# Attention scores of two heads on 64 partitions each: six products for a pair of tiles in place of four

## The chip, the cores and the metric

The kernel runs on one core of one Trainium2 chip. The metric is the device time of one execution in microseconds (us). The time before is 910.82 us, the median of three runs (909.99 to 911.43). One further execution was profiled; all views of the profile and the trace are of that one.

The engines are called as the profile calls them: PE (TensorE, matrix products; PEld is its weight load, which overlaps the products), DVE (VectorE), ACT (ScalarE), POOL (GpSimd) and SP (SyncE, which issues most DMAs). A line such as L827 is line 827 of the kernel before.

## What is computed

One encoder block over 512 tokens of width 2048: a normalised, modulated input `h`, one input projection, two token mixers side by side (dilated attention with 16 heads of 64, and a chunked gated linear attention, GLA), gates, an output projection and a last normalisation. The change touches the scores of the attention. Cut to that, the reference is:

```python
aq, ak, av = aq.reshape(hs), ak.reshape(hs), av.reshape(hs)      # 16 heads x 64
for window, dilation in ((128, 1), (512, 4), (2048, 16)):
    o_p, lse_p = dilated_window_attention(aq, ak, av, rel_bias, window, dilation)
# in it: s = q . k * 64 ** -0.5 + bias; s = where(mask, s, -1e30); p = softmax(s); o = p . v
mix_w = softmax(stack(lses))
att = einsum('pbsh,pbshe->bshe', mix_w, stack(outs))
```

The kernel folds the three patterns into one softmax: masks, bias and the multiplicity of a key are one additive row for each head (`grow`), from which a tile `g` is read at a stride.

## The kernel before, in words

**Precision.** A float32 operand is split into a high part, rounded to the product's format (fp32r), and a low part, the remainder. A product of two split operands is three products: high x high, low x high, high x low (`three`, L227 to L230).

**Stages.** First the modulation and the projection of the values, of GLA's queries and of the first two pairs of attention heads (until about 185 us). Then four projection units, "qk2", "qk4", "qk6" (queries and keys of the next four heads each) and "gk" (GLA's keys), L1255 to L1260. Beside each unit's products runs the attention of four heads, that is two pairs, whose queries and keys the stage before made. After about 440 us follow GLA, the gates and the output projection; the change does not touch those.

**Order of the work.** PE's order is the program's order, written out by hand. A unit (`unit`, L1125) has 64 ticks; a tick is one `three` of 512 columns. A list of side items, each with a place between 0 and 1, is walked along, and an item is issued when its place times 64 is reached. The other engines' order is made by the framework's scheduler from priorities, side items first.. SP works its queue of DMAs in order, so that a DMA that waits holds up those behind it.

**The attention's items** (`attention`, L798). A tile is one head `h` and one block `i` of 128 queries against 416 keys; a unit has 16 tiles. Three kinds of item:

- `score(h, i)`: two products into a PSUM tile `s` (L819, L820); two operations on DVE that add the bias and keep the running minimum (L827; the queries carry the minus sign); the exponential with its sum on ACT (L831); the reciprocal on DVE (L834); the scaling on POOL (L842). Between the minima and the reciprocal DVE gets one piece of unrelated "side work" (`beside`, L784): a sum of tokens (L1194 to L1218) or half a bias of the values (L964, L327).
- `turn(h, i)`: three transposes on PE (L857), a copy on ACT (L861) and a subtraction on DVE (L862) make the high and low part in a tile `pt`; a fourth small transpose (L870) follows for odd blocks, with L875 and L877.
- `values(h, e)`: eight products (L886) for two blocks, a copy on ACT (L889), an addition on DVE (L893).

Scores run two tiles ahead of turns, turns two ahead of values. All 40 items of a unit lie evenly on 0.8 of it, from 0.185 on (`ATT_AT`, L110), the first two and the last moved a little.

**PSUM.** Five tiles carry the tag `pj` (the projection, and L870), three the tag `pa`. Scores, turns and values draw their tiles from these three in turn: the next comes free only when the one three places back has been read.

**Queries and keys** (`qk_evict`, L757). The projection leaves two heads' queries in one PSUM tile, 64 partitions each, and their keys in another. The kernel makes for each head a tile `ks` whose one half of the partitions holds the keys' high part and whose other half holds their low part (L766, L767), and tiles `qh` and `ql` with the queries' high and low part in both halves: one half is written by ACT or DVE (L773, L775), the other is a copy by DMA across partitions (L774, L777). So a product of 128 rows is `qh . (kh + kl)`, and two products give all four terms. Keys 0 to 255 stand a second time at 512 to 767, copied by DMA (L770), since a block's window of 416 keys runs over the end.

**Bias rows.** `g_load` (L804) fetches one head's `g` (384 KB) into one of the two tiles of tag `g`; the next head's is asked for in the second score of the present head.

Of the kernel before, what the change touches and what calls it, by code (L numbers as in the profile page):

```python
# [10 lines left out]
F32 = mybir.dt.float32  # L11
# [7 lines left out]
P = 128  # L19
# [170 lines left out]
def block_kernel(ctx: ExitStack, tc: tile.TileContext, a: dict):  # L190
# [566 lines left out]
    def qk_evict(p, psq, psk):  # L757

        for j in range(2):
            own = slice(64 * j, 64 * j + 64)
            oth = slice(64 - 64 * j, 128 - 64 * j)
            ks = key_tile(2 * p + j)
            src = psk[own].rearrange("p (c a) -> p a c", a=2)
            act(by_parity(ks, own), src, AF.Copy)  # L766
            tt(by_parity(ks, oth), src, by_parity(ks.bitcast(F32), own), op=ALU.subtract)  # L767
# [30 lines left out]
    def attention(pairs):  # L798

        tiles = [(2 * p + j, i) for p in pairs for j in range(2) for i in range(4)]  # L800
# [8 lines left out]
        def score(h, i):  # L809
            def go():  # L810
                if h % 8 == 0 and i == 0:
                    cat[h // 8] = B8(f"cat{h // 8}", [4, 512])
# [6 lines left out]
                mm(ps[:, :NK], qh[:, q], ks[:, k], start=True, stop=False)  # L819
                mm(ps[:, :NK], ql[:, q], ks[:, k], start=False, stop=True)  # L820
# [12 lines left out]
                with tc.issue_after(held) if held else nullcontext():  # L833
                    nc.vector.reciprocal(st[:, 2:3], st[:, 1:2])  # L834
# [939 lines left out]
```

## Time and profile before

| what | value |
|---|---|
| median of three runs | 910.82 us |
| the profiled execution, its own time | 910.26 us |
| its span (first to last instruction) | 908.5 us |
| PE busy | 894.6 us, 98% of the span |
| DVE busy | 727.5 us, 80% |
| ACT busy | 492.9 us, 54% |
| mean granted PE clock | 0.997 of full speed |
| first and last score product | 194.8 and 435.1 us |
| moved by DMA | 241.30 MB, mean 266 GB/s |

A product is pipelined: its record lasts longer than the time after which the next one starts, so the pitch between starts, not the duration, is what a product costs in a full stream. In a row by group the numbers behind the bar are busy us, mean ns of one, and the idle time ahead of it with what ended it.

### The profile page before, as it was taken

Reading aid. Unit: us, or ns where it says so; the run is one execution under the profiler, and the core shown is the slowest. Engines: PE = TensorE matmul, PEld = TensorE weight load, DVE = VectorE, ACT = ScalarE, POOL = GpSimd, SP = SyncE. Lnnn points to the kernel's source line nnn. Section 1 sums busy time; section 2 is a strip of 40 time slices with the busy share of each in tenths; the row PEclk is TensorE's granted clock in tenths of the full one; section 3 lists DMA queues with packets and bytes.
Section 4 is the critical chain, followed back from the end, with each engine's and each line's share of the span. In section 5 each row is a group of like instructions: output and inputs, shape, how many; then the busy total and the mean of one; then the engine's idle time right before and its main releaser. Section 6 shows DMA issues by size and latency. Waiting matters only on the chain.

```text
span 908.5 us, 12576 instructions
## 1 busy us (share of the span) xinstructions
PE 894.6 (98%) x4295; PEld 746.9 (82%) x4295; DVE 727.5 (80%) x1235; ACT 492.9 (54%) x855; POOL 113.8 (13%) x203
## 2 busy tenths in 40 slices
PE   8999999999999999999999999999999999999996
PEld 6888888888888888888878888888888888888884
DVE  7988799878879888888659668495787559797797
ACT  5553533565655655655658554373654238455464
POOL 0000000023312222222100101111120100000001
PEclk9999999999999999999999999999999999999998
DMA  9999498588688898997878979778796987887863
GB/s 348 402 413 400 181 356 316 167 247 229 202 267 250 239 254 243 240 283 209 275 242 257 319 199 312 210 232 273 230 282 200 278 288 277 294 286 254 298 233 143
DMA packets 64203, 241.30 MB, mean 266 GB/s; under 512 B 8357, under 2 KB 10693, under 8 KB 54537
## 3 DMA queue, kind: packets, MB, share of 16 engines
q1 hardware_dynamic: 57378, 198.18, 61.1%
q0 software_dynamic: 6464, 42.01, 20.0%
q8 instruction: 34, 0.56, 0.2%
q10 hardware_dynamic: 296, 0.30, 0.1%
q14 instruction: 31, 0.25, 0.1%
HBM read 224.64 MB, written 51.47 MB: 304 GB/s over the span
## 4 chain that ended last, share of the span: by engine, by line
PE 92%; DVE 3%; ACT 2%; DMA 1%; issue 1%; SPq 0%; DVEq 0%; ACTq 0%
PE ps_qk L228 5%; PE ps_qk L229 5%; PE ps_qk L230 5%; PE g L230 4%; PE g L229 4%; PE g L228 4%; PE o L886 3%; PE stb L230 3%; PE stb L228 3%; PE stb L229 3%; PE ps_ag L228 3%; PE ps_ag L230 3%; PE ps_ag L229 3%; PE ps_gv_P L228 3%; PE ps_gv_P L229 3%; PE ps_gv_P L230 3%
## 5 line engine op out<-in xcount | busy, mean ns | idle before, releaser
L327 DVE CUSTOM_DVE_ANT_0 cb<-cb,sb,c_bcond 128x2048 f32<-128x2048 f32 (+1 forms) x32 | 73.4, 2295 | 0.3 <-DMA cb<-in_wm 0.3
L842 POOL TENSOR_SCALAR p<-p,st 128x416 f32<-128x416 f32 (+2 forms) x93 | 47.3, 516 | 175.2 <-DVE st L834 133.1
L831 ACT ACTIVATE p<-p,st 128x416 f32<-128x416 f32 x64 | 41.0, 641 | 39.5 <-DVE st L827 37.1
L861 ACT ACTIVATE pt<-t 128x384 fp32r<-128x384 f32 x64 | 31.2, 487 | 31.0 <-PE t L857 30.5
L428 POOL DMA_DIRECT2D T<-in_w_o x32 | 23.1, 723 | 157.9 <-ACT V2h L492 10.8
L886 PEld LDWEIGHTS o<-pt,vv 128*128 128x128 f32 x256 | 34.4, 189 | 4.2 <-DVE pt L862 1.7
L862 DVE TENSOR_TENSOR pt<-t,pt 128x384 fp32r<-128x384 f32 x64 | 35.1, 549 | 2.5 <-ACT pt L861 2.0
L886 PE MATMUL o<-pt,vv 128*128 128x256 f32 x256 | 35.9, 283 | 0.1
L857 PEld LDWEIGHTS t<-c_ident,p 128*128 128x128 f32 x192 | 24.8, 140 | 8.6
L857 PE MATMUL t<-c_ident,p 128*128 128x128 f32 x192 | 31.3, 272 | 0.0
L827 DVE CUSTOM_DVE_ANT_0 p<-s,g 128x160 f32<-128x160 f32 x64 | 23.5, 367 | 7.2 <-PE s L820 6.3
L827 DVE CUSTOM_DVE_ANT_0 p<-s,g,st 128x256 f32<-128x256 f32 x64 | 27.6, 431 | 1.6
L327 DVE CUSTOM_DVE_ANT_0 rawg<-rawg,crow,gate 128x1024 f32<-128x1024 f32 x16 | 20.4, 1280 | 4.1 <-DMA rawg<-in_wg 4.1
L820 PE MATMUL s<-ks,ql 128*128 128x416 f32 x64 | 22.5, 352 | 0.0
L819 PE MATMUL s<-ks,qh 128*128 128x416 f32 x64 | 22.5, 352 | 0.0
L1057 ACT ACTIVATE sq<-st,sc 128x256 f32<-128x256 f32 x24 | 12.2, 506 | 18.4 <-DVE st L1047 9.9
L428 POOL DMA_DIRECT2D T3V<-in_w_gv x8 | 5.5, 687 | 126.0 <-ACT qk21h L492 119.8
L1547 POOL TENSOR_SCALAR x<-x,rn 128x512 f32<-128x512 f32 x2 | 2.3, 1164 | 148.0 <-ACT rn L1536 143.6
L327 DVE CUSTOM_DVE_ANT_0 rawg<-rawg,crow,c_bcond 128x1024 f32<-128x1024 f32 x16 | 20.3, 1279 | 0.1
L877 DVE TENSOR_TENSOR pt<-r,pt 32x128 fp32r<-32x128 f32 x64 | 17.8, 279 | 1.9 <-ACT pt L875 1.3
L428 POOL DMA_DIRECT2D T<-T x16 | 9.1, 571 | 79.9 <-ACT V8h L492 12.9
L562 ACT ACTIVATE h_hi<-xt,shift 128x512 fp32r<-128x512 f32 x16 | 11.5, 719 | 12.9 <-DVE shift L327 12.9
(1660 smaller groups left out, 3129.6 us busy)
## 6 DMA issues: line engine op xcount, KB each, us to landing
cb<-in_wm SPq DMA_DIRECT2D x31, 1024.0 KB, 9.0
T<-in_w_o POOLq DMA_DIRECT2D x32, 512.0 KB, 6.6
rawg<-in_wg SPq DMA_DIRECT2D x32, 512.0 KB, 5.8
raw_O<-in_w_o SPq DMA_DIRECT2D x32, 512.0 KB, 4.4
raw_qk<-in_w_qk SPq DMA_DIRECT2D x24, 512.0 KB, 4.6
raw_O<-T SPq DMA_DIRECT2D x24, 512.0 KB, 5.0
rawb<-in_w_sb SPq DMA_DIRECT2D x16, 512.0 KB, 5.4
rawv<-in_wv SPq DMA_DIRECT2D x16, 512.0 KB, 4.4
```

Of the source, the lines that this page charges most:

```text
L228: mm(ps, lh, rh, start=first, stop=False, skip_group_check=more)
L229: mm(ps, ll, rh, start=False, stop=False, skip_group_check=more)
L230: mm(ps, lh, rl, start=False, stop=last, skip_group_check=more)
L327: return nc.vector.tensor_tensor_reduce(out=w, in0=w, in1=with_, op0=ALU.mult, op1=ALU.add, scale=1.0, scalar=init, accum_out=dst)
L428: move = nc.gpsimd.dma_start(dst, src, max_dma_last_dim=8192, **how).ins
L827: top = nc.vector.tensor_tensor_reduce(out=t[:, lo:hi], in0=ps[:, lo:hi], in1=gt[h][:, at:at + 2 * (hi - lo) - 1:2], op0=ALU.add, op1=ALU.min,
L831: act(t, t, AF.Exp, bias=st[:, 0:1], scale=-1.0, accum_out=st[:, 1:2])
L842: last["pool"] = nc.gpsimd.tensor_scalar(to, of, st[:, 2:3], 1.0, op0=ALU.mult, op1=ALU.mult).ins
L857: nc.tensor.transpose(pk[:, kt * P:kt * P + P], t[:, first_ + kt * P:first_ + kt * P + P], ident)
L861: act(hi, src, AF.Copy)
L862: tt(lo, src, hi.bitcast(F32), op=ALU.subtract)
L886: mm(po[:, :256], vv[h // 4][:, CHUNK_OF[e][c], h % 4, :], t[:, w, c, :], start=n_ == 0 and w == 0, stop=n_ == 3 and w == 1)
```

## The change

Two heads are now worked on together. `qk_evict` splits the whole PSUM tile of 128 partitions at once: `kh`, `kl`, `qh`, `ql` hold two heads, one on each half of the partitions. The keys' second copy is made from PSUM as well. No DMA copies queries or keys any more. A score item is a pair of heads and one block: six products of 64 rows, two heads in turn, into two PSUM tiles; the product low x low is no longer computed. Then the two tiles' chains follow (`chances`, which holds L821 to L843 as before).

With it the order changes: the tiles of a unit alternate between the two heads, so there are 8 score items in place of 16 and 32 items in all; values stand ahead of turns; a tile `pt` belongs to a head's parity and no longer to a half of the blocks; both heads' bias tiles are asked for together, behind the last score of the pair before; and the two last tiles that ACT scales in place of POOL are the last blocks of heads 14 and 15.

```diff
     def qk_evict(p, psq, psk):
-        for j in range(2):
-            own = slice(64 * j, 64 * j + 64)
-            oth = slice(64 - 64 * j, 128 - 64 * j)
-            ks = key_tile(2 * p + j)
-            src = psk[own].rearrange("p (c a) -> p a c", a=2)
-            act(by_parity(ks, own), src, AF.Copy)
-            tt(by_parity(ks, oth), src, by_parity(ks.bitcast(F32), own), op=ALU.subtract)
-            both = key_pair.get(p // 2) if p % 2 else ks
-            if p % 2 == 0 or j:
-                nc.sync.dma_start(both[..., 512:768].bitcast(F32), both[..., 0:256].bitcast(F32))
-            qh, ql = T2(f"qh{p}{j}", F32R), T2(f"ql{p}{j}", F32R)
-            src = psq[own, ::-1].rearrange("p (c e) -> p e c", e=2)
-            act(by_parity(qh, own), src, AF.Copy, scale=-0.125)
-            nc.sync.dma_start(qh[oth].bitcast(F32), qh[own].bitcast(F32))
-            stt(by_parity(ql, own), src, -0.125, by_parity(qh.bitcast(F32), own),
-                op0=ALU.mult, op1=ALU.subtract)
-            nc.sync.dma_start(ql[oth].bitcast(F32), ql[own].bitcast(F32))
-            stacks[2 * p + j] = [qh, ql, ks, own]
+        kh, kl = key_tile(2 * p), key_tile(2 * p + 1)
+        every = slice(0, P)
+        src = psk.rearrange("p (c a) -> p a c", a=2)
+        act(by_parity(kh, every), src, AF.Copy)
+        tt(by_parity(kl, every), src, by_parity(kh.bitcast(F32), every), op=ALU.subtract)
+        qh, ql = T2(f"qh{p}", F32R), T2(f"ql{p}", F32R)
+        of = psq[:, ::-1].rearrange("p (c e) -> p e c", e=2)
+        act(by_parity(qh, every), of, AF.Copy, scale=-0.125)
+        stt(by_parity(ql, every), of, -0.125, by_parity(qh.bitcast(F32), every),
+            op0=ALU.mult, op1=ALU.subtract)
+        act(kh[:, 512:768], src[:, 0, :], AF.Copy)
+        tt(kl[:, 512:768], src[:, 0, :], kh[:, 512:768].bitcast(F32), op=ALU.subtract)
+        stacks[p] = [qh, ql, kh, kl]
...
-        tiles = [(2 * p + j, i) for p in pairs for j in range(2) for i in range(4)]
+        tiles = [(2 * p + j, i) for p in pairs for i in range(4) for j in range(2)]
...
-        def score(h, i):
+        def score(p, i):
             def go():
...
-                if i == 1 and h != heads[-1]:
-                    g_load(h + 1)
-                qh, ql, ks, _ = stacks[h]
+                qh, ql, kh, kl = stacks[p]
                 q = slice(P * i, P * i + P)
                 k = slice(KEYS_AT[i], KEYS_AT[i] + NK)
-                ps = PA(f"s{h}{i}")
-                mm(ps[:, :NK], qh[:, q], ks[:, k], start=True, stop=False)
-                mm(ps[:, :NK], ql[:, q], ks[:, k], start=False, stop=True)
...
+                pss = [PA(f"s{2 * p + j}{i}") for j in range(2)]
+                for n_, (l, r) in enumerate(((qh, kh), (ql, kh), (qh, kl))):
+                    for j in range(2):
+                        own = slice(64 * j, 64 * j + 64)
+                        mm(pss[j][:, :NK], l[own, q], r[own, k], start=n_ == 0, stop=n_ == 2)
+                for j in range(2):
+                    chances(2 * p + j, i, pss[j])
+                if i == 3 and p != pairs[-1]:
+                    g_load(2 * p + 2)
+                    g_load(2 * p + 3)
             return go
+
+        def chances(h, i, ps):
...
-                    if (h, i) in ((15, 2), (15, 3)):
+                if h >= 14 and i == 3:
...
         def turn(h, i):
             def go():
                 e, half = divmod(i, 2)
-                if len(pts) == e:
-                    pts.append(B8(f"pt{e}", [2, 4, 256], F32R))
+                j = h % 2
+                if len(pts) == j:
+                    pts.append(B8(f"pt{j}", [2, 4, 256], F32R))
...
-                pt, t = pts[e], pr_[h, i]
+                pt, t = pts[j], pr_[h, i]
...
         for x in range(n + 4):
-            if x < n:
-                items.append(score(*tiles[x]))
-            if 2 <= x <= n + 1:
-                items.append(turn(*tiles[x - 2]))
+            if x < n and x % 2 == 0:
+                items.append(score(tiles[x][0] // 2, tiles[x][1]))
             v = x - 4
             if 0 <= v < n and tiles[v][1] % 2 == 1:
                 items.append(values(tiles[v][0], tiles[v][1] // 2))
+            if 2 <= x <= n + 1:
+                items.append(turn(*tiles[x - 2]))
         g_load(heads[0])
+        g_load(heads[1])
```

More of the change, by code (lines that the diff above doesn't have):

```diff
@@ L831, in go @@
-                act(t, t, AF.Exp, bias=st[:, 0:1], scale=-1.0, accum_out=st[:, 1:2])
-                held = beside(top)
-                with tc.issue_after(held) if held else nullcontext():
-                    nc.vector.reciprocal(st[:, 2:3], st[:, 1:2])
-                todo_ = [(t, t)]
-                if i % 2:
-                    todo_ = [(t[:, :384], t[:, :384]), (pr_[h, i - 1][:, 64:96], t[:, 384:416])]
-                for to, of in todo_:
-                    if (h, i) in ((15, 2), (15, 3)):
-                        act(to, of, AF.Copy, scale=st[:, 2:3])
-                    else:
-                        last["pool"] = nc.gpsimd.tensor_scalar(to, of, st[:, 2:3], 1.0, op0=ALU.mult, op1=ALU.mult).ins
@@ L880, in go @@
             def go():
-                t = pts[e]
+                t = pts[h % 2]
                 po = PA(f"o{h}{e}")
```

46 lines of the change are left out of this document (29 added, 17 removed).

## The prediction

> **What bounds the kernel now.** I read the page first: the busy line, then the chain that ended last.
>
> ```profile
> span 908.5 us, 12576 instructions
> PE 894.6 (98%) x4295; PEld 746.9 (82%) x4295; DVE 727.5 (80%) x1235; ACT 492.9 (54%) x855; POOL 113.8 (13%) x203
> ...
> PE 92%; DVE 3%; ACT 2%; DMA 1%; issue 1%; SPq 0%; DVEq 0%; ACTq 0%
> ```
>
> PE is 92% of the chain. A busy PE need not be one that waits for nothing, so I went to the stage that the change touches, four units with attention beside them, from about 195 to 438 us. The first row is the stretch of one of those units in which attention items run; the sum is that of eight stretches which cover 195 to 455 us.
>
> ```profile
> 265.00:309.00 44.00, 43.97 (x240) 37.51 (x239) 39.62 (x123) 25.52 (x64) 13.12 (x25) 1.00 0.87 266
> ...
> sum 260.00, PE 259.95 PEld 221.45 DVE 217.17 ACT 153.70 POOL 68.09; mean PE 32.49 PEld 27.68 DVE 27.15 ACT 19.21 POOL 8.51
> ```
>
> The columns are length, busy PE, PEld, DVE, ACT, POOL, granted clock (1.00), DMA share and GB/s. PE idles 0.05 us in 260; DVE is next, 39.62 of 44 us, 90%. Then PE's timeline, for the pitch from one product to the next, which is what a product costs in a full stream:
>
> ```profile
> 211.31 0.35 PE L819 MATMUL s<-ks,qh 128*128 128x416 f32 x1
> 211.50 0.35 PE L820 MATMUL s<-ks,ql 128*128 128x416 f32 x1
> 211.68 0.39 PE L228 MATMUL ps_qk<-h_hi,qk23h 128*128 128x512 f32 x1
> 211.91 0.39 PE L229 MATMUL ps_qk<-h_hi,qk23l 128*128 128x512 f32 x1
> 212.14 0.39 PE L230 MATMUL ps_qk<-h_lo,qk23h 128*128 128x512 f32 x1
> 212.37 0.49 PE L857 MATMUL t<-c_ident,p 128*128 128x128 f32 x3
> 212.61 0.48 PE L228 MATMUL ps_qk<-h_hi,qk23h 128*128 128x512 f32 x1
> 212.93 0.39 PE L229 MATMUL ps_qk<-h_hi,qk23l 128*128 128x512 f32 x1
> ```
>
> A score product lasts 0.35 us but the next begins 0.185 us later (211.31 to 211.68 for two). A projection product of 512 columns has a pitch of 0.23. Three transposes cost 0.33 (212.37 to 212.93 less one 0.23), 0.11 each. So PE time in this stage is the kernel's time, both ways: each 0.185 us that the scores save or add is saved or added, unless PE then starts to wait.
>
> **The change part by part.**
>
> *The products.* A pair of score tiles (two heads, one block of 128 queries) takes four products of 128 rows now and six of 64 rows after. There are 32 such pairs: 128 products become 192. The trace has no product of 64 rows, so I bound it. If two products on different halves of the rows run side by side, a pair of tiles costs 3 x 0.185 = 0.555 us instead of 4 x 0.185 = 0.74: 32 x 0.185 = 5.9 us less. If they take turns it costs 6 x 0.185 = 1.11: 11.8 us more. I take side by side. The pitch follows the columns streamed (0.185 for 416, 0.23 for 512), and two streams that use different halves of the rows carry together what one of 128 rows carries; nothing in these rows asks for a second pass. This is the weakest step; the other end stays in the range.
>
> A measurement from the Trainium skill leans the same way: "TensorE: Matmul & The Clock Gate", in Part 3, says that matmuls in distinct row groups start about 4 ns apart and run at once. By that a pair of tiles would cost 0.555 us and a few ns. No run here shows it.
>
> *The weight loads.* Six loads of 128 columns have to fit in where four were.
>
> ```profile
> L820 PEld LDWEIGHTS s<-ks,ql 128*128 128x128 f32 x64 | 12.0, 188 | 2.7
> L1278 PEld LDWEIGHTS plr<-h_hi,lrs 128*64 128x64 f32 x3 | 0.4, 135 | 0.1
> ...
> 209.67 1.10 PE L886 MATMUL o<-pt,vv 128*128 128x256 f32 x8
> 210.61 0.40 PE L228 MATMUL ps_qk<-h_hi,qk23h 128*128 128x512 f32 x1
> ```
>
> A load is 188 ns for 128 columns and 135 for 64: 53 ns for each 64, so 107 of the 188 grow with the columns. The L886 products run at a pitch of 0.94 / 8 = 0.117 us with loads as long, so a load hides behind 0.117. Two loads one after the other need 2 x 0.107 = 0.214 for each couple, above 0.185: the gain would be 32 x (0.74 - 0.642) = 3.1 us. If loads into different halves overlap, it stays 5.9. I take 5.9 and keep 3.1 as a rival.
>
> *Changes of shape.* PE goes from 128-row products to 64-row ones and back in each of 32 rounds. The only change of shape in the trace is in the columns:
>
> ```profile
> 451.56 0.39 PE L230 MATMUL ps_gv_P<-V2l,h_hi 128*128 128x512 f32 x1
> 451.79 0.40 PE L1278 MATMUL plr<-h_hi,lrs 128*64 128x512 f32 x1
> 452.03 0.39 PE L1279 MATMUL plr<-h_lo,lrs 128*64 128x512 f32 x1
> 452.26 0.39 PE L228 MATMUL ps_gv_P<-V2h,h_hi 128*128 128x512 f32 x1
> 452.48 0.39 PE L229 MATMUL ps_gv_P<-V2h,h_lo 128*128 128x512 f32 x1
> ```
>
> To 64 columns and back the pitch stays 0.23 us. I put rows at nothing too. The other end: PE lets the tail of the last product run out at each change, 0.35 - 0.185 = 0.165 us, 64 times, 10.6 us.
>
> The Trainium skill speaks for that other end: "TensorEngine Tiling (Array Packing)", Key Properties, has it that a change of tiling mode, unlike a change of tile, drains the engine. By that rule the sum would be the second rival's below; the rows above show no drain where only the columns change.
>
> *The ring of three PSUM tiles (pa).* Score, turn and values share three tiles. Now one score item takes one; after, it takes two at once, and PE, which runs in order, stops with the projection's products queued behind it if the ring is full. There are 32 items instead of 40 in 0.8 of 64 ticks: 1.6 ticks apart, a tick being three products, 0.69 us, so 1.10 us. Where a score is followed by two turns and the next score (4 rounds of 8 in a unit, 16 in all), the next score comes 3 x 1.10 + 0.555 + 0.33 + 0.44 = 4.63 us after it and needs the second head's tile back. How long that tile is held, from DVE's timeline now:
>
> ```profile
> 259.18 1.23 DVE L476 TENSOR_TENSOR qk43l<-raw_qk,qk43h 128x1024 fp32r<-128x1024 f32 x1 [2.87 <-ACT qk43h L492]
> 260.32 0.32 DVE L827 CUSTOM_DVE_ANT_0 p<-s,g 128x160 f32<-128x160 f32 x1
> ...
> 261.09 0.08 DVE L827 DVE_READ_ACCUMULATOR2_ANT st<- 128x1 f32 x1
> 261.09 0.69 DVE L1194 TENSOR_TENSOR S<-h_hi 128x512 f32<-128x512 f32 x1
> 261.70 0.42 DVE L827 CUSTOM_DVE_ANT_0 p<-s,g 128x256 f32<-128x256 f32 x1
> 262.05 0.08 DVE L827 DVE_READ_ACCUMULATOR2_ANT st<- 128x1 f32 x1
> 262.05 0.16 DVE L834 RECIPROCAL st<-st 128x1 f32<-128x1 f32 x1
> ...
> L862 DVE TENSOR_TENSOR pt<-t,pt 128x384 fp32r<-128x384 f32 x13 | 7.1, 548 | 0.3 <-ACT pt L861 0.3
> L964 DVE CUSTOM_DVE_ANT_0 rawv<-rawv,shb 128x1024 f32<-128x1024 f32 x3 | 3.7, 1220 | 0.0
> ```
>
> Products with tail 0.555 + 0.165, the first head's two biased minima 0.85 (260.32 to 261.17), its side work 0.69 or 1.22, the reciprocal 0.16, the second head's minima 0.85: 3.3 to 3.8 us, which fits in 4.63. With an L476 (1.23) and an L862 (0.55) ahead in DVE's queue it is 5.1 to 5.6, some 0.7 over. L476 comes about once a round. I let one tight round in four meet it in full: 4 x 0.7 = 2.8 us of PE waiting. The ends are 0 and 16 x 0.7 = 11.2.
>
> *The eviction of queries and keys.* Per pair of heads four copies on ACT and four subtractions on DVE over 64 partitions become two and two over 128, and one of each over 256 elements is new.
>
> ```profile
> L767 DVE TENSOR_TENSOR ks<-ps_qk,ks 64x512 fp32r<-64x512 f32 x12 | 8.3, 689 | 0.4
> L766 ACT ACTIVATE ks<-ps_qk 64x512 fp32r<-64x512 f32 x12 | 7.1, 594 | 1.6 <-DVE ks L767 1.4
> L893 DVE TENSOR_TENSOR cat<-o,oh 64x256 f32<-64x256 f32 x5 | 2.1, 416 | 0.7 <-ACT oh L889 0.6
> L889 ACT ACTIVATE oh<-o 64x256 f32<-64x256 f32 x30 | 11.4, 381 | 11.2 <-PE o L886 10.2 <-ACT pt L875 0.3
> ...
> qh<-qh SPq DMA_DIRECT2D x16, 128.0 KB, 6.0
> ql<-ql SPq DMA_DIRECT2D x16, 128.0 KB, 7.5
> ks<-ks SPq DMA_DIRECT2D x8, 128.0 KB, 7.5
> ks<-ks SPq DMA_DIRECT2D x4, 256.0 KB, 4.9
> ```
>
> DVE saves 2 x 0.689 - 0.42 = 0.96 us a pair, ACT 2 x 0.594 - 0.38 = 0.81, times eight 7.7 and 6.5 us; here I assume that 128 partitions take the time of 64, and nothing hangs on it. 44 transfers go from SP's queue. None of it is on the path: PE does not idle at the ends of units, and the first score comes some 10 ticks into a unit, about 7 us and more after the last eviction. I count nothing for it. Gain or loss here could be a tenth or two at each of four seams, within 1 us.
>
> *The bias rows (g).* Both heads' tiles now come together, into the only two tiles of that tag, behind the last score of the pair before. In mid-unit the load waits on SP for DVE's last read, with the weight loads of the projection behind it; those are fetched two to three groups of 8 ticks ahead, over 11 us, which covers it.
>
> ```profile
> g<-grow SPq DMA_DIRECT2D x16, 384.0 KB, 5.3
> ```
>
> From that score to the next lie 5 x 1.10 + 0.555 + 0.33 + 0.44 + 2 x 0.94 = 8.7 us. The first head's tile is read by 0.72 + 0.85 = 1.6 and lands at 6.9; the second's at 3.8 + 5.3 = 9.1, and it is read about 1.6 us or more into the round. It fits by 1 us or so; without that cover each of four mid-unit changes loses 1 to 2 us. I count nothing, and the range has room for it.
>
> *Sum.* The profiled execution took 910.26 us, 1.76 around its span of 908.5; the median of the runs shown is 910.82, 0.56 above it. Span: 908.5 - 5.9 + 2.8 = 905.4; with 1.76 around it 907.2; on the footing of the median 907.7 us.
>
> **The rivals.** Each on the same footing, 910.8 before.
>
> 1. *The halves take turns*: six products at 0.185, so the change does not do what "side by side" says. 910.8 + 11.8 = 922.6; PE is then slow enough that the ring does not bind. For it: no row shows two products sharing a stream time. Against it: the pitch is a matter of columns alone. It turns slower as soon as a couple costs over 0.25 us.
> 2. *The change of rows drains PE*: 10.6 - 5.9 = 4.7 more, 915.5; the ring is not waited for, since PE drains. Against it the 0.23 us around L1278; for it that rows are not columns.
> 3. *The ring takes the place of the products*: every tight round meets a full DVE queue, 11.2 - 5.9 = 5.3 more, 916.1. For it DVE's 90%; against it the 7.7 us that DVE sheds (outside these rounds) and that a wait gives DVE time. It ends slower from 0.37 us a tight round on.
> 4. *The loads set the pitch*: 3.1 less, 2.8 of waiting back, 910.5: no difference.
>
> **How the numbers follow.** A measurement of this kernel tells about 0.2% (1.8 us) from no change. My forecast, 904.9 (nothing waits) to 909.0: 0.42. Loads: 0.13. Drain: 0.10. Ring: 0.13. Turns: 0.18. What is left, mostly lost bias loads and mixtures on the slow side: 0.04. Faster by over 0.2% has the forecast and the better part of the load case: 0.45; within 0.2% the rest of that case and a half-filled ring: 0.13; slower 0.42. Both signs hold much, so the likeliest case's own range is 904.9 to 909.0; the range that holds 8 in 10 is 904.5 to 923.5, which takes in the turns.
>
> **What would show it.** Right: score products of 64 rows that start in couples a few ns apart, couples 0.185 us apart, no gap at their edges, and PE waits of under 3 us in all before score or turn. Wrong: single starts 0.185 apart (turns); couples 0.21 apart (loads); a gap of 0.165 at each edge (drain); PE waiting for DVE's L827 ahead of a score or turn (ring) or DVE's L827 waiting for a DMA (bias rows).

## The result, and the profile after

| | before | after |
|---|---|---|
| median | 910.87 us (3 runs and those beside the change) | 945.41 us (4 runs, 943.45 to 947.77) |
| ratio | | 1.0376, 95% interval 1.0364 to 1.0389 |
| the profiled execution, its span | 910.26, 908.5 us | 944.64, 942.9 us |
| scores of the first attention unit to the values' last product | 194.8 to 446.9 us | 195.8 to 478.7 us |

The change makes the kernel slower by 34.5 us, outside the range of the prediction. The page of the kernel after, its busy line and the chain that ended last:

```profile
span 942.9 us, 12569 instructions
...
PE 908.7 (96%) x4359; PEld 736.4 (78%) x4359; DVE 719.9 (76%) x1227; ACT 487.3 (52%) x848; POOL 131.3 (14%) x202
...
PE 77%; DVE 10%; DMA 6%; issue 4%; ACT 2%; POOL 1%; DVEq 0%; ACTq 0%; SPq 0%; POOLq 0%
```

PE was 92% of the chain and is 77% now; DVE comes in with 10%. The same stretch of time as in the prediction, into which less of the unit's work now falls, by windows (length, PE, PEld, DVE, ACT, POOL, clock, DMA share, GB/s):

```profile
265.00:309.00 44.00, 41.02 (x226) 31.43 (x225) 35.45 (x112) 21.93 (x55) 17.49 (x24) 1.00 0.68 208
```

PE idles 3 us of 44 where it idled 0.03, and DVE is busy *less*, 35.45 us in place of 39.62, as is ACT (21.93, 25.52); POOL is busier (17.49, 13.12) and far from full. So no engine has become full: the engines wait for each other. The granted clock is full here. Who PE waits for, in the view of waits (us in total, times, longest):

```profile
PE r L871 <- DVE pt L879: 16.7, 12, 2.5
PE t L858 <- POOL p L843: 2.3, 2, 1.2
```

L871 is the fourth, small transpose (L870 before), L879 the subtraction that reads its tile last. The second question is what the products themselves cost. PE's timeline around one score visit, with starts in the first column:

```profile
209.66 0.40 PE L230 MATMUL ps_qk<-h_lo,qk22h 128*128 128x512 f32 x1
209.99 0.46 PE L813 MATMUL s<-ks,qh 64*128 64x416 f32 x2
210.29 0.35 PE L813 MATMUL s<-ks,ql 64*128 64x416 f32 x2
210.48 0.35 PE L813 MATMUL s<-ks,qh 64*128 64x416 f32 x2
210.76 0.50 PE L228 MATMUL ps_qk<-h_hi,qk23h 128*128 128x512 f32 x1
211.09 0.39 PE L229 MATMUL ps_qk<-h_hi,qk23l 128*128 128x512 f32 x1
```

Three couples ("x2"): the two halves do run side by side (single starts lie 3 ns apart, median of 32 visits), and the third couple follows the second after 0.19. But four gaps are longer than the pitch of their products: into the visit 0.33 (209.66 to 209.99; 0.23 before the change), first to second couple 0.30 (0.19), out of it 0.28 (0.19), and the first product behind it 0.33 (0.23). Each is 0.10 too long, 0.40 a visit.

PE's weight loads show where half of this comes from:

```profile
209.44 0.19 PEld L230 LDWEIGHTS ps_qk<-h_lo,qk22h 128*128 128x128 f32 x1
209.99 0.19 PEld L813 LDWEIGHTS s<-ks,qh 64*128 64x128 f32 x2 [0.36 <-issue]
210.10 0.19 PEld L813 LDWEIGHTS s<-ks,ql 64*128 64x128 f32 x2
...
210.75 0.19 PEld L228 LDWEIGHTS ps_qk<-h_hi,qk23h 128*128 128x128 f32 x1 [0.28 <-issue]
210.86 0.19 PEld L229 LDWEIGHTS ps_qk<-h_hi,qk23l 128*128 128x128 f32 x1
```

In the stream a load runs one product ahead of its own product (L230: load at 209.44, product at 209.66). At a change of rows it starts only together with its product, 2 ns ahead (median of 32 visits; 0.23 us ahead of a visit's first product in the kernel before). The next load follows 0.11 us later, and the second product starts that much late. This is the second and the fourth of the long gaps. For the two others, into the visit and out of it, the trace shows only that neither a load nor a product of the new shape starts sooner.

**Where the 34.4 us of span went.** I added up, from the first score product to the last values product, what each gap between PE's starts exceeds the pitch of its product in a full stream (so a score visit counts whole: its products are nothing but excess).

| us | before | after |
|---|---|---|
| score visits | 24.7 | 33.2 |
| ahead of the fourth transpose (r) | 0.0 | 19.7 |
| ahead of and between other transposes (t) | 0.4 | 3.6 |
| projection, values, rest | 3.1 | 3.1 |
| sum | 28.2 | 59.6 |

31.4 of the 34.4 lie there: 8.5 in the visits and 22.9 in waits ahead of transposes. A further 2.6 arise behind the attention, mostly in the output projection; no experiment was aimed at them and they stay open. The last 0.4 is not placed.

Of the 8.5 in the visits, about 6.6 are the long gaps less the products saved (a clean visit takes 0.98 us, the four products before took 0.77). One visit that ran at half the granted clock adds 1.0. The second visit of each of the four units adds 0.2 to 0.45, about 1.3 in all: one head's first product waits there for a `pa` tile, and starts 0.16 us after DVE has read it, four times out of four (the read ends at 197.61, the product starts at 197.76). These parts are taken against the median visit and add up only roughly.

**How the wait for r arises.** PE and the others around one such wait, from the timeline of after; in brackets the idle time and what ended it:

```profile
275.71 0.49 PE L858 MATMUL t<-c_ident,p 128*128 128x128 f32 x3
...
276.02 0.69 DVE L1212 TENSOR_TENSOR S<-S,h_lo 128x512 f32<-128x512 f32 x1
276.04 0.27 PE L871 MATMUL r<-c_ident,p 128*64 128x128 f32 x1
...
277.11 1.21 DVE L967 CUSTOM_DVE_ANT_0 rawv<-rawv,shb 128x1024 f32<-128x1024 f32 x1
277.21 0.53 ACT L877 ACTIVATE pt<-r 32x128 fp32r<-32x128 f32 x2
...
277.55 0.49 PE L858 MATMUL t<-c_ident,p 128*128 128x128 f32 x3
...
278.71 0.57 DVE L879 TENSOR_TENSOR pt<-r,pt 32x128 fp32r<-32x128 f32 x2
279.31 0.56 DVE L863 TENSOR_TENSOR pt<-t,pt 128x384 fp32r<-128x384 f32 x1
...
279.42 0.27 PE L871 MATMUL r<-c_ident,p 128*64 128x128 f32 x1 [1.39 <-DVE pt L879]
```

The first head's r is written at 276.04 and its tile comes free at 279.28, 3.2 us later. The second head's turn stands one item behind (277.55) and wants the same tile 0.33 later: the projection holds four of the five `pj` tiles, so r has one. In the kernel before the same tile is wanted at this rhythm (two neighbours in its timeline):

```profile
307.56 0.27 PE L870 MATMUL r<-c_ident,p 128*64 128x128 f32 x1
...
312.06 0.27 PE L870 MATMUL r<-c_ident,p 128*64 128x128 f32 x1
```

4.5 us is the shortest distance there, up to 7.4 inside a unit. The tile is held *longer* before (median of 32: 2.7 us from r to the end of the last subtraction; 2.1 after). Only the distance differs: after, 2.1 to 4.2 us within a pair, of which part is the wait itself, and 11 to 14 between pairs. The demand per unit is the same; it comes in bursts of two.

### The profile page after: what moved, and what is told of

Read it like the earlier page. It is cut to its first block, busy times and chain, and to the rows that moved or that the text cites. A ratio compares the mean times of both kernels' runs of the same rounds, so it can differ in the third digit from the quotient of the medians.

```text
span 942.9 us, 12569 instructions
## 1 busy us (share of the span) xinstructions
PE 908.7 (96%) x4359; PEld 736.4 (78%) x4359; DVE 719.9 (76%) x1227; ACT 487.3 (52%) x848; POOL 131.3 (14%) x202
## 4 chain that ended last, share of the span: by engine, by line
PE 77%; DVE 10%; DMA 6%; issue 4%; ACT 2%; POOL 1%; DVEq 0%; ACTq 0%; SPq 0%; POOLq 0%
PE ps_qk L228 4%; PE ps_qk L230 3%; PE ps_qk L229 3%; PE g L230 3%; PE stb L230 3%; PE g L228 3%; PE g L229 3%; PE stb L228 3%; PE stb L229 3%; PE ps_ag L230 3%; PE ps_ag L229 3%; PE ps_ag L228 3%; PE ps_gv_P L230 3%; PE ps_gv_P L228 3%; PE ps_gv_P L229 3%
## 5 line engine op out<-in xcount | busy, mean ns | idle before, releaser
L843 POOL TENSOR_SCALAR p<-p,st 128x384 f32<-128x384 f32 (+2 forms) x92 | 64.6, 711 | 178.3 <-DVE st L835 136.6
L862 ACT ACTIVATE pt<-t 128x384 fp32r<-128x384 f32 x64 | 31.3, 489 | 18.5 <-PE t L858 17.4
L828 DVE CUSTOM_DVE_ANT_0 p<-s,g 128x160 f32<-128x160 f32 (+1 forms) x64 | 22.5, 371 | 16.4 <-PE s L813 14.1
L813 PE MATMUL s<-ks,qh 64*128 64x416 f32 x128 | 27.7, 407 | 0.0
L828 DVE CUSTOM_DVE_ANT_0 p<-s,g,st 128x256 f32<-128x256 f32 (+1 forms) x64 | 27.1, 427 | 0.3
L871 PE MATMUL r<-c_ident,p 128*64 128x128 f32 x32 | 8.8, 276 | 17.0 <-DVE pt L879 16.7
L813 PEld LDWEIGHTS s<-ks,qh 64*128 64x128 f32 x128 | 13.4, 187 | 12.5 <-issue 11.4
L895 DVE TENSOR_TENSOR cat<-o,oh 64x256 f32<-64x256 f32 x32 | 13.3, 416 | 11.4 <-ACT oh L891 11.1
L891 ACT ACTIVATE oh<-o 64x256 f32<-64x256 f32 x32 | 12.2, 382 | 18.9 <-PE o L888 18.6
```

Of the source, the lines that this page charges most:

```text
L813: mm(pss[j][:, :NK], l[own, q], r[own, k], start=n_ == 0, stop=n_ == 2)
L828: top = nc.vector.tensor_tensor_reduce(out=t[:, lo:hi], in0=ps[:, lo:hi], in1=gt[h][:, at:at + 2 * (hi - lo) - 1:2], op0=ALU.add, op1=ALU.min,
L843: last["pool"] = nc.gpsimd.tensor_scalar(to, of, st[:, 2:3], 1.0, op0=ALU.mult, op1=ALU.mult).ins
L862: act(hi, src, AF.Copy)
```

## The experiments

Three theories at first. **Tile (R)**: the single tile for r is the loss. **Burst** (rival B in the expectations of e5 to e8, theory C in later ones): two heads' equal steps follow each other at once, the engines' queues are worked in order, and the slack between score, turn and values doesn't cover it; the tile is only where it shows. **Products (D)**: the loss is the 64-row products with their edges. The diffs are short, and against the kernel after unless said otherwise.

### Order or products: e2 and e3

e2 has the order of after, with the products, copies and `qk_evict` of before:

```diff
-                for n_, (l, r) in enumerate(((qh, kh), (ql, kh), (qh, kl))):
-                    for j in range(2):
...
+                for j in range(2):
+                    qh, ql, ks, _ = stacks[2 * p + j]
+                    mm(pss[j][:, :NK], qh[:, q], ks[:, k], start=True, stop=False)
+                    mm(pss[j][:, :NK], ql[:, q], ks[:, k], start=False, stop=True)
```

> The changed order of items, with the eviction and the four products of 128 rows of the kernel before (copies by DMA too). Theory R: the order alone carries the loss, 19.7 us of waiting for pj, about 5 for the pa ring at scores, 3 for turns; without the 3.1 us that the six products cost net: 936 to 943 us. Theory D: without 64-row products the loss goes, 910 to 914 us.

Measured 942.50 us (1.0328, 1.0287 to 1.037): 31 us of the loss without a product of 64 rows; 21.9 us ahead of r. Products as the main cause fell. e3 is the other half: the order of before, three products of 64 rows a tile, one head a visit, 64 visits.

```diff
-                mm(ps[:, :NK], qh[:, q], ks[:, k], start=True, stop=False)
-                mm(ps[:, :NK], ql[:, q], ks[:, k], start=False, stop=True)
+                for n_, (l, r) in enumerate(((qh, kh), (ql, kh), (qh, kl))):
+                    mm(ps[:, :NK], l[own, q], r[own, k], start=n_ == 0, stop=n_ == 2)
```

> The order of the kernel before (one head's tile for each score item), with the changed eviction and three products of 64 rows for each tile: nothing side by side, and 64 visits to 64-row products in place of 32. If a visit costs 0.30 us at its edges, as the trace of the changed kernel shows (0.097 in, 0.094 + 0.110 out), a tile takes 3 x 0.185 + 0.30 = 0.86 us in place of 0.38: 31 us more than before, 940 to 944 us. If the edges are a result of waits and cost nothing by themselves: 3 x 0.185 - 0.37 = 0.185 us a tile, 12 us more, 921 to 925 us.

949.31 us (1.0416, 1.0397 to 1.0436), more than either expected. PE waits for nothing ahead of a transpose; all of it is in the visits, 62.1 us against 24.7. One visit:

```profile
201.35 0.39 PE L230 MATMUL ps_qk<-h_lo,qk21h 128*128 128x512 f32 x1
201.67 0.46 PE L814 MATMUL s<-ks,qh 64*128 64x416 f32 x1
201.97 0.34 PE L814 MATMUL s<-ks,ql 64*128 64x416 f32 x1
202.16 0.35 PE L814 MATMUL s<-ks,qh 64*128 64x416 f32 x1
202.44 0.50 PE L228 MATMUL ps_qk<-h_hi,qk22h 128*128 128x512 f32 x1
202.78 0.39 PE L229 MATMUL ps_qk<-h_hi,qk22l 128*128 128x512 f32 x1
```

It takes as long as the visit with both heads above (1.43 us from the product ahead of it to the second one behind it): the second head is free. And the four long gaps are the same. Twice as many visits cost twice the edges.

### The tile: e1, e5, e7, e6, e8

e1 puts r into the unused columns of its turn's own `pa` tile, behind the copies:

```diff
-            pk = PJ(f"r{h}{e}")
-            nc.tensor.transpose(pk[:64, :P], pr_.pop((h, 2 * e))[:, 64:128], ident)
+            nc.tensor.transpose(pk[:64, 3 * P:], pr_.pop((h, 2 * e))[:, 64:128], ident)
```

> The changed kernel with one edit: the fourth small transpose of a turn (L871) goes into the free columns 384 to 511 of the turn's own PSUM tile and no longer into a tile of tag pj. Theory R (the single free pj tile is what both heads' fourth transposes queue for): the 19.7 us that PE spends between L858 and L871 go, some of it comes back as waits for the pa ring, whose tile is now held longer; time 924 to 930 us. Theory D (the change of rows drains PE and the waits only follow from it): the wait moves to the next place, 938 to 945 us.

997.43 us (1.0934, 1.0895 to 1.0972), a new wait of the edit's own making: r now writes a tile that ACT and DVE are still reading. Its waits:

```profile
PE t L870 <- DVE pt L863: 43.5, 26, 2.8
PE t L870 <- DVE st L835: 13.0, 6, 2.7
```

That says nothing on R. e5 mends it: the same tile, but r right behind the three transposes, ahead of the copies.

> The changed kernel with the fourth small transpose in the free columns of the turn's own PSUM tile, and issued right behind the three large ones, ahead of the copies that read the tile (in e1 it stood behind them and PE waited for those, 57 us of DVE work on the same tile). Theory R (one free pj tile is what PE waits for): the 19.7 us between L858 and L871 go; turns of odd blocks hold their pa tile up to 1 us longer, which gives some waits back: 924 to 934 us. Rival B (DVE and ACT are behind with the two heads' chains, and the tile is only where it shows): the wait moves to scores and turns, 939 to 950 us.

946.04 us (1.0378, 1.0361 to 1.0395). The wait for r is gone, and stands elsewhere:

```profile
PE s L813 <- DVE pt L879: 14.7, 12, 2.9
```

The next score products wait for the `pa` tile instead, since turns now hold it to the last subtraction. That R alone is the loss fell: taking r out of its tile moves the wait. The edit also makes the turn hold its `pa` tile longer, so it is no test with one tile more; e15 below is. e7 is e5 with the products of before:

> The changed order with the four products of 128 rows of the kernel before, and the fourth transpose early in the turn's own tile as in e5. Theory R: e2's 21.9 us of waiting for the pj tile go, 920 to 930 us; and e5 less this run gives what the six products cost net when that wait is gone: 3 us by the edges of 0.30 us less the steps saved. Rival B: 936 to 946 us.

937.20 us (1.0281, 1.026 to 1.0302): the wait as in e5, `s` for L885 (L879 there), 13.4 us. e6 leaves the tile alone and puts the score item behind the first head's turn, so that the two turns are two items apart; e8 does that and e5.

```diff
+            if 2 <= x <= n + 1:
+                items.append(turn(*tiles[x - 2]))
             if x < n and x % 2 == 0:
                 items.append(score(tiles[x][0] // 2, tiles[x][1]))
...
-            if 2 <= x <= n + 1:
-                items.append(turn(*tiles[x - 2]))
```

> The changed kernel with one shift in the order of items: a score stands behind the first head's turn instead of ahead of it, so that the two heads' turns are two items apart instead of one, about 2.8 us instead of 1.5. Theory R: PE's wait for the free pj tile falls from 19.7 us to under 8, the rest of the loss stays: 930 to 938 us. Rival B: DVE and ACT have as much to do, the wait goes elsewhere: 942 to 950 us.

> Both edits of e5 and e6 on the changed kernel. Theory R: nothing waits for a pj tile and the pa ring has more time: 918 to 928 us, which leaves the 3 us of the products and a few of ring waits over the kernel before. Rival B: 936 us or more.

e6: 941.37 us (1.0322, 1.03 to 1.0344); r costs 3.0 us, but the first turn comes too soon after its score:

```profile
PE t L858 <- POOL p L843: 11.8, 6, 2.9
```

e8: 949.20 us (1.0413, 1.0385 to 1.0442), the same wait. Each cure of one place shows the next one: burst.

### One head's products together: e4

```diff
-                for n_, (l, r) in enumerate(((qh, kh), (ql, kh), (qh, kl))):
-                    for j in range(2):
+                for j in range(2):
+                    for n_, (l, r) in enumerate(((qh, kh), (ql, kh), (qh, kl))):
```

> The changed kernel with the six products of a pair of tiles in the order head by head (three of one, then three of the other) instead of in turn. If products on the two halves of the rows run side by side only when they stand next to each other, only the third of one head and the first of the other do: five steps of 0.185 in place of three, 0.37 us more in each of 32 rounds, 11.8 us, less what PE would have waited anyway: 950 to 958 us. If the order among the six does not matter: 944 to 947 us.

960.89 us (1.0541, 1.0523 to 1.0559), but not as expected: a clean visit is unchanged, and the two halves still start together:

```profile
210.19 0.47 PE L813 MATMUL s<-ks,qh 64*128 64x416 f32 x2
210.49 0.36 PE L813 MATMUL s<-ks,ql 64*128 64x416 f32 x2
210.68 0.35 PE L813 MATMUL s<-ks,qh 64*128 64x416 f32 x2
```

Most of the loss over after has another source. The visits sum to 37.7 us in place of 33.2, the gaps between the projection's products to 6.9 in place of 2.0, and 6 us more stand ahead of r. What the first two grew by, 9.4 of 15.5 us, lies in spells in which PE's granted clock stood at half, 30.7 us of them within the attention (3.4 in after, none before). In one of them, by windows:

```profile
353.00:356.00 3.00, 3.00 (x11) 1.66 (x10) 0.53 (x1) 0.00 (x0) 0.11 (x1) 0.50 0.89 287
```

There the projection's pitch is 0.43 us (median) in place of 0.23, and the six visits that such a spell touches take 1.7 to 2.0 us in place of 0.98. What brought the clock down isn't shown. DVE and ACT also run in another order than in after, and the 6 us ahead of r stay open.

### Side work on DVE: e9, e11, e12

In the stall above DVE has two pieces of side work (L1212, L967: 1.9 us) between the turn's transposes and the subtraction that PE waits for. So a fourth theory, **side work (S)**. e9 moves each piece behind a turn's last subtraction; the second diff is e11's, which shrinks the pieces (the sums of tokens all in the manner of the first line) and so leaves out most of those sums and of the values' bias.

```diff
-            held = beside(top)
-            with tc.issue_after(held) if held else nullcontext():
-                nc.vector.reciprocal(st[:, 2:3], st[:, 1:2])
+            nc.vector.reciprocal(st[:, 2:3], st[:, 1:2])
...
                 if half:
-                    rest(h, e)
+                    done = rest(h, e)
+                beside(done)
             return go
```

```diff
-            return tt(made[n + "3"], h_part(h, th, kh, kp), h_part(h, 1, 0, kp), op=ALU.subtract).ins
+            return tt(made[n + "3"][:, :, :32], h_part(h, th, kh, kp)[:, :, :32], h_part(h, 1, 0, kp)[:, :, :32], op=ALU.subtract).ins
...
-            return cond_sum(vbias[:, m:m + 1], raw, shb[0][:, 1024:], vbias0[:, m:m + 1]).ins
+            return cond_sum(vbias[:, m:m + 1], raw[:, :64], shb[0][:, 1024:1088], vbias0[:, m:m + 1]).ins
```

> The changed kernel with each piece of side work on VectorE moved from between a tile's minima and its reciprocal to behind a turn's last subtraction; the amount of work is the same. Theory S (side work: the two pieces that belong to the pair's two tiles, 0.69 to 1.23 us each, stand in VectorE's order between the pair's minima and the subtractions of the turn that PE waits for): the waits of PE for VectorE's subtractions fall from 19.7 us to under 7, and the time to 918 to 932 us. Theory C (the two heads' chains of minima, exponential, reciprocal and turn are too long for the round, whatever stands between): the waits stay above 14 us, 938 to 948 us.

> The changed kernel with the side work cut to a small part: the sums of tokens work on 64 of 512 columns and the halves of the bias on 64 of 1024 (the rest is filled with zeros by POOL or left out, so the gates and the values' bias are not the reference's). VectorE has some 40 us less to do beside attention. Theory S: PE's waits for VectorE before scores and transposes fall from 28 us to under 8, 914 to 926 us. Theory C: they stay above 18 us, 934 to 944 us.

e9: 938.92 us (1.0307, 1.0282 to 1.0332), 18.5 us still ahead of r. e11: 950.11 us (1.041, 1.0381 to 1.0439), 20.2 ahead of r. That time is above what either theory expected: POOL, which scales the tiles, also fills the parts left out, and this may hide a gain. The wait ahead of r, which S said would go, stays in both. Moving the side work gave back 6.5 us of 34.5; S fell as the main cause.

### Slack: e10, e16, e15, e14

e10 is e6 with turns and values a pair of tiles later:

```diff
-            v = x - 4
+            v = x - 6
...
-                items.append(turn(*tiles[x - 2]))
+                items.append(turn(*tiles[x - 4]))
```

> The changed kernel with the pair's products between its two turns, and turns a whole pair of tiles further behind their scores (values too). Where the pair's products stood between the turns, PE waited 13.6 us for the scaling on POOL; with a round more of slack that wait must be gone. Theory C (too little slack between score and turn): waits of PE before transposes and scores in all fall under 10 us, 920 to 932 us. Theory S (VectorE's side work ahead of the turn's subtractions): it stands there as before, so PE waits as long, at another place, 936 to 950 us.

929.54 us (1.0207, 1.0179 to 1.0234): r 0.8, t 5.1. And the test from the other side, e16: the kernel *before*, with nothing changed but turns one tile behind their scores in place of two (values three).

```diff
-            if 2 <= x <= n + 1:
-                items.append(turn(*tiles[x - 2]))
-            v = x - 4
+            if 1 <= x <= n:
+                items.append(turn(*tiles[x - 1]))
+            v = x - 3
```

> The kernel before with less slack: a turn follows its score after one tile in place of two, values after three in place of four; nothing else is changed. Theory C: slack between score and turn is what the order of before has and the changed order lacks; PE then waits before transposes for POOL and VectorE, 925 to 950 us. If slack is not what matters, within 3 us of before.

941.09 us (1.0329, 1.0314 to 1.0345). Its waits:

```profile
PE t L857 <- POOL p L842: 15.8, 14, 1.9
```

26.9 us ahead of transposes, visits 24.8 as before. The kernel before loses what the change loses as soon as it lacks slack. e15 gives after, at its old lag, a fourth PSUM tile for the burst (e5, and the odd head's transposes in the fifth `pj` tile):

```diff
-                pk = PA(f"t{h}{i}")
+                pk = (PJ if j else PA)(f"t{h}{i}")
```

> The changed kernel with the fourth transpose in its turn's own tile, ahead of the copies, and the odd head's transposes in the fifth tile of the projection's tag, so that scores, turns and values of a pair draw from four PSUM tiles in place of three, with no change of the lag. Theory P (too few PSUM tiles for two heads' burst): PE's waits fall from 27 us to under 12, 920 to 932 us (946.0 us with three tiles). Theory C (the chain from score to turn is too long for the round, PSUM only shows it): the wait moves once more, 938 to 948 us.

925.41 us (1.0149, 1.0132 to 1.0166). Here the burst theory's own expectation (theory C: the wait moves once more, 938 to 948) missed, and too few PSUM tiles (theory P) was met. So the tiles are more than the place where the burst shows: one more tile or more distance each takes most of it away, and taking r out of its tile alone (e5) doesn't. In e10, DVE's view of waits shows what is left:

```profile
DVE p L828 <- DMA g<-grow: 8.9, 5, 3.6
```

e14 is e10 with four tiles for the bias rows, asked for in the pair's second block.

```diff
-    t2 = mid.enter_context(tc.tile_pool(name="t2", bufs=15))
-    gp = mid.enter_context(tc.tile_pool(name="gp", bufs=2))
+    t2 = mid.enter_context(tc.tile_pool(name="t2", bufs=11))
+    gp = mid.enter_context(tc.tile_pool(name="gp", bufs=4))
...
-                if i == 3 and p != pairs[-1]:
+                if i == 1 and p != pairs[-1]:
```

> The longer lag and the pair's products between the two turns, with four tiles for the bias rows in place of two, asked for two rounds earlier (11 tiles t2 in place of 15 make the room). Theory G (both heads' bias rows together come late, VectorE's minima wait for the DMA 8.9 us in all and PE for VectorE behind them): that wait goes, 923 to 927 us. If PE does not feel it: 928 to 932 us.

920.29 us (1.0101, 1.0086 to 1.0116), 25 us off the loss with the change's products and evictions untouched. The stretch of a unit and PE's longest wait in the attention:

```profile
265.00:309.00 44.00, 44.00 (x242) 34.48 (x242) 39.32 (x125) 26.01 (x64) 17.99 (x28) 1.00 0.68 208
```

```profile
PE r L871 <- DVE pt L879: 0.3, 1, 0.3
```

PE idles nowhere and DVE is as busy as before (39.32; 39.62). What is left against before is the visits, 32.9 us against 24.7: 8.2 of the 9.0 us. Clean visits are 6.6 of these; most of the rest is, as in after, the second visit of each unit (1.26 to 1.29 us).

Two combinations did worse than their parts. e12 is e9 and e10 together; e13 is e10 with the products and copies of before.

> All three at once, with the whole work: side work behind the turns, the pair's products between the two turns, turns a pair of tiles later. If only side work matters, the time is that of the kernel with the side work moved; if only slack matters, that of the one with the longer lag; if each hides the other, this one alone is near 914 to 922 us (the products' own loss of some 3 us over the kernel before, and seams). A time above 935 us would say that neither is the cause.

935.36 us (1.0265, 1.0247 to 1.0284): just above the 935 us over which, by its expectation, neither side work nor slack would be the cause. The trace gives another reading: with the side work gone from between, DVE's reciprocal waits for ACT's exponential 14.6 us, and r waits 5.9 again. That this new wait alone makes the time is not shown.

> The longer lag and the pair's products between the two turns, but with the products and copies of the kernel before (four products of 128 rows for the pair of tiles). Against the same order with products of 64 rows (929.5 us): if the 64-row products cost what their clean rounds show, 0.205 us more a pair of tiles, it is 6.5 us faster, 921 to 925 us; if they cost nothing, 927 to 932 us.

929.69 us (1.0212, 1.0178 to 1.0246). The time says "nothing", but it can't be read so: in the profiled execution (934.82 us) the visits sum to 29.8, and DVE waits 11.8 us for bias rows, behind which t waits 12.1.

### The visits: e17 and e18

e17 puts two blocks of the pair into one visit, twelve products, 16 visits (with e14's bias tiles, e10's lag, and r in its turn's tile as in e5).

```diff
-                pss = [PA(f"s{2 * p + j}{i}") for j in range(2)]
...
+                for i in (2 * e, 2 * e + 1):
...
+                        pss[i, j] = (PJ if i % 2 and j else PA)(f"s{2 * p + j}{i}")
...
+            if x < n and x % 4 == 0:
+                items.append(score(tiles[x][0] // 2, tiles[x][1] // 2))
```

> Two blocks of a pair of heads in one visit: twelve products of 64 rows one after the other, 16 visits in place of 32; four tiles for the bias rows, turns four tiles behind their scores, the fourth transpose in its turn's own tile, the fourth score tile in the projection's tag. Theory V (the 64-row products lose their gain at the edges of a visit, 0.40 us each time, whatever its length): against the kernel with six products a visit and no waits (920.3 us) 16 x 0.40 = 6.4 us less, 913 to 916 us, if no new wait comes. If the loss is per product, 919 to 922 us. If four score tiles at once make PE wait, more than 925 us, and then the gaps at the visits' edges in the trace tell, not the time.

One visit of it:

```profile
214.59 0.40 PE L230 MATMUL ps_qk<-h_lo,qk23h 128*128 128x512 f32 x1
214.92 0.46 PE L816 MATMUL s<-ks,qh 64*128 64x416 f32 x2
215.21 0.35 PE L816 MATMUL s<-ks,ql 64*128 64x416 f32 x2
215.40 0.54 PE L816 MATMUL s<-ks,qh 64*128 64x416 f32 x4
215.77 0.36 PE L816 MATMUL s<-ks,ql 64*128 64x416 f32 x2
215.96 0.36 PE L816 MATMUL s<-ks,qh 64*128 64x416 f32 x2
216.25 0.50 PE L228 MATMUL ps_qk<-h_hi,qk23h 128*128 128x512 f32 x1
216.58 0.39 PE L229 MATMUL ps_qk<-h_hi,qk23l 128*128 128x512 f32 x1
```

932.46 us (1.022, 1.0198 to 1.0242), since four score tiles at once bring new waits (13 us ahead of and within values, 8 ahead of transposes). The trace still answers: the same four long gaps, once a visit ("x4" is two couples, the last of the first block and the first of the second), and the six couples otherwise 0.18 to 0.19 apart; the visits sum to 24.5 us, 8.4 less than in e14, where theory V had 6.4 (the 2 beyond are what e14's visits cost above clean ones). The loss is at the edges. At 16 visits the 64-row products cost what the 128-row ones do (24.7).

e18 is e15 with the products and copies of before.

> The kernel with four PSUM tiles for a pair's burst (925.4 us), but with the products and copies of the kernel before, four of 128 rows a pair of tiles. If products of 64 rows cost 6.5 to 8 us more in 32 visits, as their clean rounds show, 917 to 920 us; if they cost nothing, 924 to 927 us.

929.42 us (1.0205, 1.0187 to 1.0222), no gain: visits of which most are clean, but some wait up to 2 us, once for a copied `ql` (DMA), and 8.5 us ahead of and within values. Neither this time nor e13's isolates the products. Their visits do: a clean one takes 0.76 us in both, with products of 128 rows, against 0.97 to 0.98 in e14 and e15. So do the gaps of e3, e14 and e17.

No run beats the kernel before; with a clean visit at 0.98 us a pair of tiles against 0.77, none of 32 visits could.

## Why the prediction was wrong, point by point

- **Bound.** That PE's time is the kernel's time held both ways. The use made of DVE's 90% misled: I looked for a full engine, and the loss came with PE, DVE and ACT all less busy.
- **The products, side by side.** Right: single starts 3 ns apart in a couple, 0.19 from couple to couple.
- **The weight loads.** Right inside a visit: 0.18 to 0.19 between couples, not 0.214, and rival 4 fell. Wrong at its edges: the step took it that a load always hides behind the product ahead, and at a change of rows it doesn't, for 0.11 us each time.
- **Changes of shape.** Failed. Put at nothing from a change of columns; a change of rows costs 0.40 us a visit, 32 times, 12.9 us. Where the prediction's other end had 0.165 at each of two edges, it is 0.10 at each of four gaps. Products and edges together: +8.2 us (e14) in place of -5.9. Rival 2 had a cost of this kind, at +4.7. The Trainium skill, "TensorEngine Tiling (Array Packing)", Key Properties, says that a change of tiling mode drains the engine. The trace agrees in that such a change is paid for, at the price just given; it shows no drain as such (the first score product starts 0.07 us ahead of the end of the record before it).
- **The ring of three PSUM tiles.** Failed, and the largest miss, by what it left out. For the demand that it priced, the score's second tile, it is near in size by luck: PE waits about 1.3 us for it in all, where 2.8 were predicted, but in the second visit of each unit, 1.6 us behind the first, and not in the rounds with two turns between that the step worked with. It looked at this one demand alone, and the waits of the turns stood at nothing without a reason. Ahead of transposes 22.9 us more are waited, 19.7 of them for the tile of the fourth transpose, which is named in the description and priced nowhere; behind it, as e5 and e6 show, the turns' tiles and POOL's scaling are as short. What the step should have asked of every buffer is the distance between two demands after the reordering, not the demand per round. Its own rival 3 had a mechanism of this kind, at 916, for the wrong tile and with half of the waits (11.2 us).
- **Eviction, copies.** Nothing on PE's path, as counted: the projection's gaps sum to 1.9 before and 2.0 after. DVE's busy time fell by 7.6 us and ACT's by 5.6, close to the 7.7 and 6.5 counted.
- **Bias rows.** Nothing in after, as counted, but only because PE's other waits gave them time: when those go (e10) DVE waits 8.9 us for them, and the step that takes this away (e14) brings 9.2 us, a little over the 4 to 8 us that the prediction named for lost cover.
- **Sum.** -5.9 + 2.8 predicted; 8.5 + 22.9 + 2.6 measured, 34.0 of 34.4. The steps that failed are the price of the edges and the waits ahead of the turns, both put at nothing.

## What to carry to other kernels

Before reordering, list for every buffer and engine queue the distance between successive demands and the time each is held; if two equal steps move next to each other, the shortest distance counts, even if the number of demands stays. Where a wait goes and shows up at another place, don't mend place by place: add slack (a longer lag, another tile) to the whole chain, and give a well-tuned kernel less slack to see how much it lives on. Products on half the rows run two for one, but a visit has a fixed price, here 0.40 us, so a visit has to save more than that.

## What the runs showed of the hardware

- A change from 128 to 64 rows and back stretches four gaps by 0.10 us each, the same for three, six or twelve products in the visit (e3, after, e17). Two of the four go with weight loads that start 2 ns ahead of their product in place of 0.23 us, and 0.11 us apart; for the other two no run shows why.
- Products on the two halves of the rows started together even where the program has three of one head ahead of three of the other (e4: starts 10 ns apart): so far as PE kept the order written in the edit, starts on different halves need not follow the order of the program.
- In some runs PE's granted clock stood at half for spells of 3.4 us or a multiple of it: 30.7 us within the attention in e4 and in e1, 3.4 in after, none before, in e3, e14 and e18. In the spells of e4 and e1 the projection's pitch is 0.43 us, and the growth of its gaps (1.9 before, 6.9 in e4, 6.7 in e1) lies there. The runs with most of it have many waits of PE, but after has 19.7 us of waits ahead of r and one spell; what sets them off no run shows.
- POOL's scaling took longer with nothing changed in it (the 128 x 416 one 648 ns before, 891 after, 750 in e14). Its cause was not looked for.
